# A hybrid decoder layer on one core: query rotation on VectorE alone, its copy on ScalarE, and projection work moved between stages

## The chip, the cores and the metric

The kernel runs on 1 core of one Trainium2 chip. Its time is the device time of one execution in microseconds (us). Five engines work side by side: TensorE (PE in the rows, its weight loads PEld), VectorE (DVE), ScalarE (ACT), GpSimd (POOL) and SyncE (SP, which only issues DMAs here). Each takes its own instructions in the order in which the program wrote them, and semaphores tie the engines together.

## The reference

One decoder layer over x of 512 tokens by 1024 features, all in float32. Cut to what matters here:

```
h    = rmsnorm(x, norm1_w);  proj = h @ w_in            # split into mq,mk,mv,mo,mi,mf,nq,kc..vw,ng,gm,gn
qk   = silu(causal_dwconv(concat(mq, mk)))              # 4 taps
hm   = rmsnorm(mlstm_chunkwise(mq, mk, mv, ...)) * sigmoid(mo)        # 4 heads
qn   = rope(rmsnorm(nq per head, q_norm_w))             # 8 heads x 64; the same for kc, ks, kw
on   = gated sum of compressed, selected and window attention (qn, k.., v..)
y    = sigmoid(gm + b0) * (hm @ w_up_m) + sigmoid(gn + b1) * (on @ w_up_n)
x    = x + y @ w_out
out  = x + (gelu(dwconv(a)) * v) @ ffn_w_down,   a, v = split(rmsnorm(x) @ ffn_w_up)
```

`rope(x)` takes the two halves x1, x2 of a head and gives x1*cos - x2*sin and x2*cos + x1*sin.

## The kernel before

Tokens are worked in four tiles of 128 (t = 0 to 3). Every float32 product is made of three matmuls over rounded halves (high x high, high x low, low x high), so one 128x512 piece of a projection is three matmuls of 512 columns. Such a triple is called a block here. Weights come from memory by SyncE into two buffers (`raw`), and are split into four rotating buffers (`whl`): ScalarE copies the high half (L88); the low half is a VectorE subtraction (L94), or, for A, gm, mo, mqk and gn, a second ScalarE copy (L91) and an accumulating DMA that GpSimd issues (L92). Each call of `ensure` issues these for one half chunk of weights.

The order is written out by hand. The attention and the mLSTM are a chain of small steps; between them stand calls `fill(ns)`, which take blocks out of one generator (`proj_stream`: the projections C, A = queries, MV, gm, mo, mqk, gn) until their nominal price, 650 ns a block, has paid the given number. A debt is carried on. The numbers come from a table, `PLAN`, read by `FL(key, default)`. `fill.until(done, flag)` takes blocks until a projection has been evacuated, and sets the debt to zero. A block that a `fill` takes early is missing later: the sum of blocks is fixed. A block also issues what hangs on its place in the stream: the weight splits of a half chunk three ahead, and evacuations (`after`, `tick`).

The places that the change touches, in time order:

- **Query tiles.** When A is done, `rope_norm` makes the scale of the query heads. Then for each tile: `rope` (L679 scale, L683 twice for the swapped half products with the sine, L686 product with the cosine, L687 sum, and a duplicate made by `cp`, L233 on ScalarE or L235 on VectorE) writes `qdup`; `q_transposes` (L846 on PE into `pq`, L848 on ScalarE and L849 on VectorE into `QS`) uses it. `rope_q(t + 1)` is issued right behind the transposes of tile t, and then `fill(z16_t)`. Keys in PLAN: `p_S1q*` and `p_dupq*` choose the engine (2 GpSimd, 1 VectorE, 0 VectorE for the product and ScalarE for the copy).
- **The rows of the mLSTM's gates** (`rows_b`), woven between attention heads; its last piece transposes them into `uop` (L1082).
- **After attention**: the convolved `mqk` is put through sigmoid (L1233), split into `mq` (L1240, L1243), then the sigmoids of `mo` (L1247) and `gm` (L1252), each with fills behind it; then ScalarE loads the function table for exponentials and logarithms (L1254).
- **mLSTM heads** h = 0 to 3: `mls_s` (scores, L1094 to L1104), `mls_e` (L1113), `mls_x` (exponential L1119, mask on GpSimd L1123), `mls_m` (L1128), `mls_b` (L1136 onwards, PE tile `mo`), `mls_c` (transposes `mhT` L1165, then L1166 to L1168). Fills `ms0`, `mb*`, `mc*`, `md*` stand between them; `mb3` is large enough to empty the stream.

Of the kernel before, what the change touches and what calls it, by code (L numbers as in the profile page):

```python
# [12 lines left out]
LNEXP = "natural_log_exp_and_others"  # L13
# [84 lines left out]
def bcast(ap, n):  # L98
# [3 lines left out]


PLAN = {
# [12 lines left out]
    "p_sc21": 0, "p_sc30": 0, "p_sc31": 1, "poolA": 2, "poolC": 0, "poolGM": 2, "poolGN": 2, "poolMO": 2,  # L117
    "poolMQK": 2, "poolMV": 0, "poolUM": 0, "poolUN": 2, "poolWO": 0, "q2_eb": 1, "q2_ex0": 0, "q2_ex1": 0,
# [8 lines left out]
}  # L127
# [1 line left out]
def FL(key, default):  # L129
    return PLAN.get(key, default)  # L130
# [30 lines left out]
def body(ctx, tc, I, out, dbg=None):  # L161
    nc = tc.nc
    act, dve, pe, pool = nc.scalar, nc.vector, nc.tensor, nc.gpsimd
# [24 lines left out]
    def sm(shape, name, bufs=2, dt=F32):  # L188
        return small.tile(shape, dt, name=name, tag=name, bufs=bufs)
# [7 lines left out]
    def page(name, dt=F32):  # L197
        return ar.tile([P, 2048], dt, name=name, tag="pg", bufs=PG)
# [7 lines left out]
    def s4(name, dt=F32):  # L206
        return ar.tile([P, 1024], dt, name=name, tag="s4", bufs=6)
# [7 lines left out]
    def pt(name):  # L215
        return ps.tile([P, 512], F32, name=name, tag="pt", bufs=1)
# [4 lines left out]
    def v4(tl):  # L221
        return tl[:, :2048].rearrange("p (k t) -> p k t", t=S)
# [520 lines left out]
    def proj_stream():  # L743
        yield from tok_group(T_C, 288, tok_accs("aC"), evac_c, "C")
        yield from tok_group(T_A, 512, tok_accs("aA"), evac_a, "A")
        T["mv1"] = lpage("mv1").rearrange("p (t h c) -> p t h c", t=NT, h=4)
        pool.memset(T["mv1"][:, :, :, P:P + 1], 1.0)
        yield from tok_group(T_MV, 512, tok_accs("aV"), evac_mv, "MV")
        T["gm"] = [v4(opage(f"gm{i}")) for i in range(2)]
        yield from feat_group(F_GM, gate_evac("gm", 0), "gm", "GM")  # L750
        T["mo"] = v4(page("mo"))
        yield from feat_group(F_MO, evac_mo, "mo", "MO")
        yield from feat_group(F_MQK, evac_conv, "mqk", "MQK")
        T["gn"] = [v4(page(f"gn{i}")) for i in range(2)]
        yield from feat_group(F_GN, gate_evac("gn", 8), "gn", "GN")

    fill = Filler(proj_stream(), flush)
# [271 lines left out]
    def rows_b():  # L1029
        ir, fr, t1, t2 = T["rows"]  # L1030

        act.activation(t1, fr, AF.Abs)
        act.activation(t1, t1, AF.Exp, scale=-1.0)
        dve.tensor_scalar(t2, fr, 0.0, None, op0=ALU.min)
        yield
        act.activation(t1, t1, AF.Ln, bias=1.0)
        yield
        dve.tensor_sub(fr, t2, t1)
        on = onesf[0:4, :]
        for c in range(NT):  # L1040
            q = slice(c * P, (c + 1) * P)
            dve.tensor_tensor_scan(t2[:, q], on, fr[:, q], 0.0, ALU.mult, ALU.add)
        yield
        dve.tensor_sub(ir, ir, t2)
        mc = sm([4, 4], "mc", 1)
        for c in range(NT):
            q = slice(c * P, (c + 1) * P)
            dve.tensor_tensor_scan(fr[:, q], on, ir[:, q], mc[:, c:c + 1] if c else 0.0, ALU.mult, ALU.max)
            if c + 1 < NT:
                e = (c + 1) * P - 1  # L1050
                dve.tensor_add(mc[:, c + 1:c + 2], t2[:, e:e + 1], fr[:, e:e + 1])
        yield

        dve.tensor_add(t1, t2, fr)
        R3 = s4("mrowC", F32R)
        nH, nL = R3[0:4, 0:512], R3[32:36, 0:512]
        pool.tensor_scalar(R3[0:32, 0:512].rearrange("p (a c) -> p a c", a=4),
                           onesf[0:32, :].rearrange("p (o c) -> p o c", o=1).to_broadcast([32, 4, P]), 0.0, None,
                           op0=ALU.mult)
        dve.tensor_scalar(fr, fr, -1.0, None, op0=ALU.mult)  # L1060
        dve.tensor_copy(nH, fr)
        dve.tensor_sub(nL, fr, nH)
        T["nHL"] = R3[0:36, 0:512]
        yield "R4"

        R4 = vst[:, 1024:1792]
        n = 0
        T["urow"] = []
        for k, (i, j) in enumerate(pairs):
            if i == j:  # L1070
                cur = ir[:, j * P:(j + 1) * P]
            else:
                new = R4[0:4, n * P:(n + 1) * P]
                n += 1
                dve.tensor_scalar(new, cur, t2[:, i * P - 1:i * P], None, op0=ALU.add)
                cur = new
            T["urow"].append(cur)

        yield
        p = pt("uop")  # L1080
        for k in range(len(pairs)):
            pe.transpose(p[:, k * 4:k * 4 + 4], T["urow"][k], ident[0:4, 0:4])  # L1082
        for t in range(NT):
            pe.transpose(p[:, 40 + t * 4:44 + t * 4], T["rows"][2][:, t * P:(t + 1) * P], ident[0:4, 0:4])
        dve.tensor_copy(uoc, p[:, 0:40])
        act.activation(emc, p[:, 40:56], AF.Exp, scale=-1.0)

    def mls_s(h):
        r0 = slice((h % 2) * 64, (h % 2) * 64 + 64)
        mq = T["mq"][h // 2][r0]  # L1090
        A = psS(f"mA{h}")
        B = psS(f"mB{h}")
        mb = B[:, 0:512]
        pe.matmul(mb, sel[:, h, :], T["nHL"], start=True, stop=True)  # L1094
        at = [A[:, 0:512], A[:, 512:896], B[:, 768:1024], B[:, 512:768]]
        for j in range(NT):
            ks = slice(j * P, (j + 1) * P)
            kh, kl = mq[:, 1, ks], mq[:, 3, ks]

            q0 = min(j, NT - 2) * P  # L1100
            qh, ql = mq[:, 0, q0:], mq[:, 2, q0:]
            pe.matmul(at[j], kh, qh, start=True, stop=False)
            pe.matmul(at[j], kh, ql, start=False, stop=False)
            pe.matmul(at[j], kl, qh, start=False, stop=True)  # L1104
        return A[:, 0:896], B[:, 640:1024], mb

    def mls_e(h, sc):
        mb = sc[2]
        EA, EB = s4(f"EA{h}"), s4(f"EB{h}")
        et = [EA[:, 0:512], EA[:, 512:896], EB[:, 128:384], EB[:, 0:128]]  # L1110
        for k, (i, j) in enumerate(pairs):
            e = et[j][:, (i - j) * P:(i - j + 1) * P]
            dve.tensor_scalar(e, mb[:, i * P:(i + 1) * P], uoc[:, k * 4 + h:k * 4 + h + 1], 0.0,  # L1113
                              op0=ALU.add, op1=ALU.min)
        return EA[:, 0:896], EB[:, 0:384], et

    def mls_x(ee):
        EA, EB, et = ee
        act.activation(EA, EA, AF.Exp)  # L1119
        act.activation(EB, EB, AF.Exp)  # L1120
        for j in range(NT):
            e = et[j][:, 0:P]
            pool.affine_select(e, e, pattern=[[1, P]], compare_op=ALU.is_ge, fill=0.0, base=0,  # L1123
                               channel_multiplier=-1)
# [124 lines left out]
    for i in range(2):  # L1249
        for z in range(2):  # L1250
            g = T["gm"][i][:, 2 * z:2 * z + 2, :]
            act.activation(g, g, AF.Sigmoid)  # L1252
            fill(FL("z26", 1300))
    act.preload_act_table_set(LNEXP)  # L1254
    T["hmH"] = v4(page("hmH", F32R))
    sc = mls_s(0)
    ee = mls_e(0, sc)
    mls_x(ee)
    fill(FL("ms0", 5000))
    mls_m(sc, ee)  # L1260
    for h in range(4):
        if h < 3:
# [5 lines left out]
        if h == 3:  # L1268
            fill.until(done, "GN")
            fill = Filler(up_group(F_UN, T["onH"], T["onL"], evac_un, "un", "UN"), flush)  # L1270
# [33 lines left out]
    fill = Filler(up_group(F_UM, T["hmH"], T["hmL"], evac_um, "um", "UM", psS), flush)  # L1304
# [336 lines left out]
```

## Time and profile before

| what | us |
|---|---|
| median of 3 runs (800.81 to 802.07) | 801.13 |
| the profiled execution's own time | 799.94 |
| its span in the trace | 798.2 |
| PE busy in the span | 776.9 (97%) |
| PEld busy | 640.9 |
| DVE busy | 469.7 |
| ACT busy | 373.0 |
| POOL busy | 211.1 |

PE counts as busy from the start of a matmul to its modelled end, and matmuls overlap, so the 97% says that PE is seldom without work, not that every cycle is used. The times of waits are read from the list of waits, which says for which engine an instruction waited last.

### The profile page before, as it was taken

What the parts mean: (1) busy time and instruction counts of PE and PEld (TensorE: products, weight loads), DVE (VectorE), ACT (ScalarE), POOL (GpSimd) and SP (SyncE); (2) the same over time, 40 slices, a digit from 0 to 9 for tenths busy, and PEclk for the clock granted to TensorE, in tenths of its full rate; (3) what the DMA queues carried; (4) which work ended last, traced back from release to release, by engine and by line L of the source; (5) the groups of instructions that cost most, each with busy time, mean ns of one, the idle gap of its engine ahead of it and who ended that gap; (6) DMA issues with size and microseconds to landing.
All of it is one profiled execution on the core that took longest, in us unless ns stands there. A gap on an engine that the chain in (4) does not pass through costs nothing.

```text
span 798.2 us, 10535 instructions
## 1 busy us (share of the span) xinstructions
PE 776.9 (97%) x4037; PEld 640.9 (80%) x4037; DVE 469.7 (59%) x825; ACT 373.0 (47%) x629; POOL 211.1 (26%) x219
## 2 busy tenths in 40 slices
PE   8999989999999999988999999999999999999998
PEld 5897878778788878866778998888888888888886
DVE  5476875686565654534764545555545544466865
ACT  6353546645565596571343343343343343355541
POOL 5320121220111122121000009855554444200600
PEclk9999999999999999999999999999999999999999
DMA  7884158665555567348343427675454444485472
GB/s 234 290 222 133 25 135 132 109 113 96 106 106 107 106 106 129 83 106 263 105 151 125 148 106 290 241 260 209 182 188 181 188 158 159 168 306 177 144 233 93
DMA packets 94371, 127.98 MB, mean 160 GB/s; under 512 B 6479, under 2 KB 73199, under 8 KB 92912
## 3 DMA queue, kind: packets, MB, share of 16 engines
q1 hardware_dynamic: 63054, 91.64, 34.3%
q0 software_dynamic: 31264, 35.66, 21.6%
q8 instruction: 32, 0.52, 0.3%
q14 instruction: 19, 0.16, 0.1%
q10 hardware_dynamic: 2, 0.00, 0.0%
HBM read 94.79 MB, written 15.73 MB: 138 GB/s over the span
## 4 chain that ended last, share of the span: by engine, by line
PE 79%; DVE 9%; ACT 6%; DMA 3%; issue 2%; SPq 0%; DVEq 0%; ACTq 0%
PE ff L1356 10%; PE ff L1357 10%; PE ff L1358 10%; PE P L426 4%; PE P L427 4%; PE P L425 4%; PE on L946 2%; PE ptp L935 2%; PE wo L425 2%; PE wo L426 2%; PE wo L427 2%; PE gm L487 1%; PE gm L489 1%; PE gm L488 1%; PE sp L905 1%
## 5 line engine op out<-in xcount | busy, mean ns | idle before, releaser
L94 DVE TENSOR_TENSOR whl<-raw,whl 128x1024 fp32r<-128x1024 f32 (+1 forms) x110 | 138.9, 1276 | 146.7 <-ACT whl L88 146.7
L88 ACT ACTIVATE whl<-raw 128x1024 fp32r<-128x1024 f32 (+2 forms) x144 | 144.8, 1013 | 125.7 <-PE ff L1358 57.0
L1356 PE MATMUL ff<-h2H,whl 128*128 128x512 f32 (+1 forms) x384 | 142.8, 372 | 0.0
L1357 PE MATMUL ff<-h2L,whl 128*128 128x512 f32 (+1 forms) x384 | 142.6, 371 | 0.0
L1358 PE MATMUL ff<-h2H,whl 128*128 128x512 f32 (+1 forms) x384 | 142.6, 371 | 0.0
L92 POOL DMA_DIRECT2D whl<-raw x32 | 46.2, 1444 | 198.5 <-ACT whl L91 190.3
L1358 PEld LDWEIGHTS ff<-h2H,whl 128*128 128x128 f32 x384 | 72.3, 188 | 12.6
L1356 PEld LDWEIGHTS ff<-h2H,whl 128*128 128x128 f32 x384 | 72.3, 188 | 12.5
L1357 PEld LDWEIGHTS ff<-h2L,whl 128*128 128x128 f32 x384 | 72.3, 188 | 12.3
L920 ACT ACTIVATE P<-sp,nmx 128x128 f32<-128x128 f32 (+3 forms) x64 | 33.1, 524 | 36.7 <-DVE nmx L911 36.4
L1408 ACT ACTIVATE ct<-ct 128x512 f32<-128x512 f32 x22 | 14.0, 634 | 54.4 <-DVE ct L1406 54.4
L911 DVE TENSOR_REDUCE nmx<-sp 128x2 f32<-128x256 f32 (+3 forms) x32 | 26.2, 818 | 17.9 <-PE sp L908 17.8
L426 PE MATMUL P<-whl,g 128*128 128x512 f32 x88 | 34.2, 389 | 0.0
L427 PE MATMUL P<-whl,g 128*128 128x512 f32 x88 | 34.2, 389 | 0.0
L425 PE MATMUL P<-whl,g 128*128 128x512 f32 x88 | 34.2, 389 | 0.0
L1406 DVE SCALAR_TENSOR_TENSOR ct<-ff,vcol,ct 128x511 f32<-128x511 f32 (+1 forms) x44 | 32.8, 744 | 2.5 <-ACT ct L1404 1.7
L91 ACT ACTIVATE whl<-raw 128x1024 fp32r<-128x1024 f32 x32 | 33.6, 1050 | 0.0
L1414 ACT ACTIVATE g<-ct 128x512 fp32r<-128x512 f32 x22 | 13.9, 634 | 37.0 <-DVE ct L1418 21.9
L235 DVE COPY P<-ptp 128x256 f32<-128x256 f32 (+1 forms) x32 | 17.7, 554 | 19.3 <-PE ptp L935 19.2
L1415 DVE TENSOR_TENSOR g<-ct,g 128x512 fp32r<-128x512 f32 x22 | 15.4, 699 | 22.0 <-ACT g L1414 22.0
L425 PE MATMUL wo<-whl,yH 128*128 128x512 f32 x64 | 25.2, 394 | 1.8 <-DVE gm L1299 1.8
L487 PE MATMUL gm<-hTH,whl 128*128 128x512 f32 x64 | 26.6, 416 | 0.0
(400 smaller groups left out, 1788.6 us busy)
## 6 DMA issues: line engine op xcount, KB each, us to landing
raw<-in_ffn_w_up_dram SPq DMA_DIRECT2D x22, 1024.0 KB, 5.0
raw<-in_w_in_dram SPq DMA_DIRECT2D x16, 1024.0 KB, 5.0
whl<-raw POOLq DMA_DIRECT2D x32, 512.0 KB, 5.7
st<-in_ffn_w_down_dram SPq DMA_DIRECT2D x11, 1024.0 KB, 6.9
td<-st POOLq DMA_DIRECT2D x11, 1024.0 KB, 4.1
raw<-td SPq DMA_DIRECT2D x22, 512.0 KB, 5.4
raw<-in_ffn_w_down_dram SPq DMA_DIRECT2D x11, 512.0 KB, 4.4
raw<-in_w_out_dram SPq DMA_DIRECT2D x4, 1024.0 KB, 11.0
```

Of the source, the lines that this page charges most:

```text
L88: nc.scalar.activation(h, src, AF.Copy)
L91: nc.scalar.activation(l, src, AF.Copy, scale=-1.0)
L92: nc.gpsimd.dma_start(l, src, accum_op=ALU.add)
L94: (nc.gpsimd if n in self.on_pool else nc.vector).tensor_sub(l, src, h)
L425: pe.matmul(o, aH, bH, start=start, stop=False)
L426: pe.matmul(o, aH, bL, start=False, stop=False)
L427: pe.matmul(o, aL, bH, start=False, stop=stop)
L487: pe.matmul(acc, H[:, k, :], hh, start=(k == 0), stop=False)
L920: act.activation(Pv[:, y], sv[:, y], AF.Exp, bias=nmx[:, y:y + 1], accum_out=den[:, y:y + 1])
L1356: pe.matmul(acc[:, a:b], H[:, k, :], hh, start=(k == 0), stop=False)
L1357: pe.matmul(acc[:, a:b], H[:, k, :], hl, start=False, stop=False)
L1358: pe.matmul(acc[:, a:b], L[:, k, :], hh, start=False, stop=(k == KD - 1))
```

## The change

Numbers of PLAN and three places of code. In PLAN: the evacuation of query tile 2 goes from VectorE to ScalarE (`e_a2` 1 to 0); the second sine product of all query tiles from GpSimd to VectorE (`p_S1q0` to `p_S1q3`, 2 to 0); the duplicate of tiles 0 to 2 from VectorE to ScalarE (`p_dupq0` to `p_dupq2`, 1 to 0; tile 3 had it there); the fills around the query tiles grow (`z14` 5850 to 6500, `z16_0` 4225 to 4875, `z16_1` 3250 to 4550, `z16_2` 4875 to 5525); the fills behind the mLSTM's heads shrink (`md0` 3950 to 3300, `md1` 3625 to 2600, `md2` 15275 to 0). In code: a `fill(650)` ahead of the transposes of `uop`; the table load for the exponentials goes from ahead of `mls_s(0)` to behind the first half of fill `ms0`, and `mls_x` of head 0 with it.

```
-    "mc0": 4675, "mc1": 5000, "mc2": 5000, "mc3": 11500, "md0": 3950, "md1": 3625, "md2": 15275, "ms0": 6300,
+    "mc0": 4675, "mc1": 5000, "mc2": 5000, "mc3": 11500, "md0": 3300, "md1": 2600, "md2": 0, "ms0": 6300,
...
-    "z13": 650, "z14": 5850, "z16_0": 4225, "z16_1": 3250, "z16_2": 4875, "z16_3": 2925, "z18": 1300, "z18a": 1950,
+    "z13": 650, "z14": 6500, "z16_0": 4875, "z16_1": 4550, "z16_2": 5525, "z16_3": 2925, "z18": 1300, "z18a": 1950,
...
         yield
+        fill(650)
         p = pt("uop")
...
-    act.preload_act_table_set(LNEXP)
     T["hmH"] = v4(page("hmH", F32R))
     sc = mls_s(0)
     ee = mls_e(0, sc)
+    fill(FL("ms0", 5000) / 2)
+    act.preload_act_table_set(LNEXP)
     mls_x(ee)
-    fill(FL("ms0", 5000))
+    fill(FL("ms0", 5000) / 2)
     mls_m(sc, ee)
```

What this does to the order of PE, counted in blocks (triples of matmuls), before and after: 16 and 17 ahead of the transposes of query tile 0 (from the last key transposes), 7 and 8 behind them, 5 and 7 behind those of tile 1, 7 and 8 behind those of tile 2; one block more ahead of `uop`; 18 and 12 between the last attention product and `mls_s(0)`; 10 and 10 between `mls_s(0)` and the first product of head 0; 7 and 7 ahead of the transposes `mhT` of head 0, 6 and 5 behind them; 8 and 8, 6 and 5 for head 1; 8 and 7, 4 and 7 for head 2. The other counts are the same.

The first place is ScalarE around query tiles 0 and 1: `qdup` is a tile's rotated queries, `whl` a half chunk of weights being split, `pq` the transposes in PSUM. Before:

```order
L383 ACTIVATE rs_l_974<-rs_l_974 128x32
L88 ACTIVATE whl_991<-raw_740 128x1024
L88 ACTIVATE whl_1020<-raw_910 128x1024
L91 ACTIVATE whl_1020<-raw_910 128x1024
L848 ACTIVATE QS_859<-pq_1027 128x512
L848 ACTIVATE QS_859<-pq_1034 128x512
L848 ACTIVATE QS_859<-pq_1070 128x512
L848 ACTIVATE QS_859<-pq_1077 128x512
L233 ACTIVATE vst<-sc_1092 128x256
L88 ACTIVATE whl_1104<-raw_910 128x1024
L91 ACTIVATE whl_1104<-raw_910 128x1024
```

The same place after:

```order
L383 ACTIVATE rs_l_974<-rs_l_974 128x32
L233 ACTIVATE qdup_983<-qdup_983 128x8x64
L88 ACTIVATE whl_991<-raw_740 128x1024
L88 ACTIVATE whl_1020<-raw_910 128x1024
L91 ACTIVATE whl_1020<-raw_910 128x1024
L848 ACTIVATE QS_859<-pq_1030 128x512
L848 ACTIVATE QS_859<-pq_1037 128x512
L233 ACTIVATE qdup_1044<-qdup_1044 128x8x64
L88 ACTIVATE whl_1070<-raw_910 128x1024
L91 ACTIVATE whl_1070<-raw_910 128x1024
L848 ACTIVATE QS_859<-pq_1080 128x512
L848 ACTIVATE QS_859<-pq_1087 128x512
```

The copy of each tile now stands ahead of the weight splits of the fill that follows it, and those ahead of the copies L848 of the same tile's transposes. Tile 2 reads likewise, with the score copy `vst<-sc` and two splits between.

The second place is ScalarE where attention ends: `onH` is the last output of attention, `cv` the convolution input of the mLSTM, `cs` its sigmoid. Before:

```order
L233 ACTIVATE P_7_2700<-ptp_7_1_2757 128x512
L956 ACTIVATE onH<-on_2378 128x4x128
L728 ACTIVATE cv_2731<-mqk_2727,vcol 128x512
L1233 ACT_TABLE_LOAD
L1233 ACTIVATE cs_2814<-cv_2522 128x1024
```

After:

```order
L728 ACTIVATE cv_2675<-mqk_2671,vcol 128x512
L233 ACTIVATE P_7_2730<-ptp_7_1_2779 128x512
L956 ACTIVATE onH<-on_2402 128x4x128
L1234 ACT_TABLE_LOAD
L1234 ACTIVATE cs_2814<-cv_2458 128x1024
```

The last evacuation of `mqk` now stands inside attention, and the table load directly behind `onH`. What follows it, up to the sigmoids of `gm`, is the same in both.

The third place is ScalarE at the exponential of head 0 (`EA`, `EB`), behind the sigmoids of `gm`. Before:

```order
L1252 ACTIVATE gm_1200<-gm_1200 128x1024 x2
L1254 ACT_TABLE_LOAD
L1119 ACTIVATE EA_2896<-EA_2896 128x896
L1120 ACTIVATE EB_2897<-EB_2897 128x384
L718 ACTIVATE gn_2793<-gn_2834,vcol 128x512
L88 ACTIVATE whl_2931<-raw_2733 128x1024
```

After:

```order
L1253 ACTIVATE gm_1180<-gm_1180 128x1024 x2
L718 ACTIVATE gn_2769<-gn_2834,vcol 128x512
L1259 ACT_TABLE_LOAD
L1120 ACTIVATE EA_2895<-EA_2895 128x896
L1121 ACTIVATE EB_2896<-EB_2896 128x384
L88 ACTIVATE whl_2931<-raw_2677 128x1024
```

One evacuation of `gn` went ahead of the table load and the two exponentials.

## Rows read from the trace of the kernel before

**Rows 1.** Busy time by stretch: engines, then clock, DMA share, GB/s.

```profile
280.00:300.00 20.00, 19.37 (x89) 15.33 (x88) 11.20 (x21) 19.96 (x24) 4.16 (x6) 1.00 0.61 106
...
376.00:404.00 28.00, 22.95 (x92) 17.94 (x91) 21.71 (x30) 7.83 (x12) 0.00 (x0) 0.94 0.22 75
```

**Rows 2.** Waits of PE: us in total, times, longest.

```profile
PE pq L846 <- DVE qdup L235: 1.8, 3, 1.0
...
PE gn L487 <- ACT gn L718: 0.6, 1, 0.6
PE mo L1136 <- DVE EA L1128: 0.6, 1, 0.6
PE pq L846 <- ACT qdup L233: 0.6, 1, 0.6
PE uop L1082 <- DVE P L235: 0.5, 1, 0.5
```

**Rows 3.** Line 686: duration ns min/median/max, first and last start.

```profile
L686 DVE TENSOR_TENSOR rtq<-qraw,tab x4: 1223/1228/1230, 93.4 to 112.8; 128x512 f32<-128x512 f32 x4
...
L686 DVE TENSOR_TENSOR rtk<-kraw,tab x1: 685/685/685, 67.8 to 67.8; 128x512 f32<-128x512 f32 x1
```

**Rows 4.** Timeline of POOL in query tile 1: start, us, instruction, idle before.

```profile
99.51 0.96 POOL L683 TENSOR_TENSOR rtq<-qraw,tab 128x256 f32<-128x256 f32 x1 [3.14 <-DVE qraw L679]
```

**Rows 5.** Timeline of DVE: a key rotation, then query tile 1.

```profile
66.43 0.69 DVE L679 TENSOR_TENSOR kraw<-kraw,rrs 128x512 f32<-128x512 f32 x1
...
68.55 0.69 DVE L687 TENSOR_TENSOR kdup<-rtk 128x512 f32<-128x512 f32 x1
...
98.73 0.69 DVE L679 TENSOR_TENSOR qraw<-qraw,rrs 128x512 f32<-128x512 f32 x1
...
99.80 1.22 DVE L686 TENSOR_TENSOR rtq<-qraw,tab 128x512 f32<-128x512 f32 x1
101.12 0.69 DVE L687 TENSOR_TENSOR qdup<-rtq 128x512 f32<-128x512 f32 x1
```

**Rows 6.** Timeline of ACT around the query tiles.

```profile
91.31 2.20 ACT L88 ACTIVATE whl<-raw 128x1024 fp32r<-128x1024 f32 x2
...
96.78 1.09 ACT L848 ACTIVATE QS<-pq 128x512 fp32r<-128x512 f32 x2 [2.32 <-PE pq L846]
...
104.86 1.05 ACT L88 ACTIVATE whl<-raw 128x1024 fp32r<-128x1024 f32 x1
105.81 1.05 ACT L91 ACTIVATE whl<-raw 128x1024 fp32r<-128x1024 f32 x1
...
114.84 0.63 ACT L233 ACTIVATE qdup<-qdup 128x512 f32<-128x512 f32 x1 [3.98 <-DVE qdup L687]
```

**Rows 7.** Timeline of PE: transposes of query tiles 0, 1 and 3.

```profile
96.12 1.06 PE L846 MATMUL pq<-ident,qdup 128*128 128x128 f32 x8 [0.31 <-DVE qdup L235]
...
102.43 1.06 PE L846 MATMUL pq<-ident,qdup 128*128 128x128 f32 x8 [0.46 <-DVE qdup L235]
...
115.52 1.09 PE L846 MATMUL pq<-ident,qdup 128*128 128x128 f32 x8 [0.57 <-ACT qdup L233]
```

**Rows 8.** Timeline of ACT from the end of attention to head 0.

```profile
276.67 0.60 ACT L956 ACTIVATE onH<-on 128x512 fp32r<-128x512 f32 x1 [2.00 <-PE on L946]
...
279.75 1.28 ACT L1233 ACT_TABLE_LOAD   x1
...
296.52 0.95 ACT L1119 ACTIVATE EA<-EA 128x896 f32<-128x896 f32 x1
...
297.79 0.67 ACT L718 ACTIVATE gn<-gn,vcol 128x512 f32<-128x512 f32 x1
```

**Rows 9.** Timeline of PE there: first block, head 0's scores, its products.

```profile
276.55 0.50 PE L487 MATMUL mqk<-hTH,whl 128*128 128x512 f32 x1
...
289.06 0.50 PE L1094 MATMUL mB<-mrowC,sel 36*128 36x512 f32 x1
...
299.37 0.46 PE L1136 MATMUL mo<-mv,EA 128*128 128x129 f32 x2
```

6 rows, old and new, of the table PLAN are left out of this document.

## The prediction

> **What bounds the kernel now.** I read the busy times first: PE is busy nearly throughout, so the kernel can only change by what PE waits, since the change neither adds nor removes a matmul. The list of waits comes second. In the stretches that the change touches, PE waits 1.8 and 0.6 us for the rotated queries, 0.5 us at `uop`, 0.6 us for an evacuation of `gn`, and 0.6 us for the exponentials of head 3 [rows 2]: 4.1 us in all, which is the most that can be won there. Third come the timelines, to see which engine ends last at each of these waits. Two things are to be seen. At the query tiles a loop runs through three engines: PE transposes, ScalarE copies (L848), VectorE subtracts and rotates the next tile, a copy makes the duplicate, PE transposes again [rows 5 to 7]. And behind attention ScalarE is the full engine: 19.96 of 20 us from 280 to 300 [rows 1], with PE just keeping pace.
>
> A block (three matmuls) costs 0.695 us: 18 blocks lie between 276.55 and 289.06 [rows 9].
>
> **Rotation on VectorE.** VectorE's product L686 takes 1.23 us in the query tiles and 0.685 us in the key rotation that leaves GpSimd out [rows 3]; in tile 1 it starts at 99.80 while GpSimd's half product runs from 99.51 to 100.47 [rows 4, 5]. GpSimd's half goes to VectorE. The row for the result is the key rotation: 66.43 to 68.55 + 0.69 = 69.24, so 2.81 us, against 98.73 to 101.81, 3.08 us, for the query tile [rows 5]. Saved: 0.27 us a tile.
>
> The Trainium skill (SBUF — State Buffer, the vocabulary entry on the shared port pair) says that GpSimd and VectorE lock a port pair for a whole instruction and the loser stands still. By that L686 would end at 100.47 + 0.685 = 101.16; the row ends at 101.02, 0.14 us sooner. Had the rule its full price, the removal would be worth 0.41 us a tile instead of 0.27 and the total some 0.4 us lower; I go by the rows.
>
> **The copy on ScalarE.** Tile 3 has it already: the copy starts at 114.84, takes 0.63, and PE starts at 115.52, so 0.68 us from copy to transposes, and 0.72 with the hop to ScalarE. Tile 1 with VectorE's copy: rotation done at 101.81, PE at 102.43, 0.62 us [rows 5 to 7]. Added: 0.10 us a tile.
>
> What counts more is what is queued behind it. ScalarE takes its instructions in order, and a copy that waits for the rotation now holds the weight splits written after it; the order shows them between the copy and L848 of the same tile. Before, three splits of tile 0 ran from 91.31 on, while VectorE rotated, and ScalarE then stood idle until 96.78; the next two ran at 104.86 and 105.81, behind L848 of tile 1 and off the loop [rows 6]. A split costs 0.95 us start to start [rows 6]. From L848 to the next rotation takes 98.73 - 96.78 = 1.95 us [rows 5, 6].
>
> Tile 0: its transposes started at 96.12 with VectorE's copy; by the two steps above the copy is done 0.27 sooner and 0.10 later, near 95.85. PE comes one block later than its arrival now, 96.12 - 0.31 + 0.69 = 96.5, and does not wait. ScalarE splits three times: 95.85 + 2.85 = 98.70, where L848 begins, almost 2 us later than now. Then 1.95 + 2.81 + 0.72 = 5.48 us to the next transposes: 104.2. Tile 1, two splits: 104.15 + 1.90 + 5.48 = 111.5. Tile 2, two splits and the score copy (0.3, an estimate from half of the 0.63 row, which moves twice as much): 111.5 + 2.2 + 5.48 = 119.2. In the kernel before, tile 3 is transposed at 115.52; the four blocks added from tile 0 on and one before it are 5 x 0.695 = 3.5 us of work done earlier, so 119.0 would be no loss. **Term: +0.2 us.** Bounds: -2.4 if all query waits go [rows 2], which needs the splits off the loop; +0.9 if a split costs the 1.05 us of a whole row [rows 6]. I take the value near the start-to-start row.
>
> The evacuation of tile 2 on ScalarE is costed at nothing: it takes the place of one of two VectorE copies ahead of `rope_norm`, and ScalarE's four squares and VectorE's four sums behind it overlap. If that cover failed it would be one 0.63 us copy [rows 6] on the loop's start, within the bound above.
>
> **`uop`.** One block ahead of its transposes gives VectorE's copy 0.69 us, and 0.5 was waited [rows 2]. **Term: -0.5 us** (0 if something else holds it).
>
> **From attention to head 0.** Six blocks fewer stand between the last attention product and `mls_s(0)` (18 to 12), since five went to the query tiles and one to `uop`. PE therefore asks for head 0's products 6 x 0.695 = 4.2 us sooner, counted from 276.55. What must be ready is ScalarE's: two sigmoids of `cv`, `mq`, `mo`, `gm`, the table load, EA. Before, the chain starts with the load at 279.75, behind the evacuation of the last `mqk`; after, that evacuation lies inside attention, and the load follows `onH`, which ends at 276.67 + 0.60 = 277.27 [rows 8]. So the chain starts 2.5 us sooner. Splits, sigmoids and copies in it are the same. At its end one evacuation of `gn` (0.67 us [rows 8]) now goes ahead of the load and EA: EA comes 2.48 - 0.67 = 1.8 us sooner, near 294.7. Head 0's products follow EA by 299.37 - 296.52 = 2.85 us [rows 8, 9], through GpSimd's mask and VectorE's product, so they start near 297.6. PE alone could be there at 299.37 - 4.2 - 0.6 = 294.6; the 0.6 us wait for `gn` goes, and one of 3 us in all takes its place, split between the scores (which need `mq`) and the products. 4.2 us of work left this stretch, and it gets 1.8 us shorter. **Term: +2.4 us.** Bounds: -0.6 (ScalarE keeps pace and the `gn` wait goes) and +4.2 (the chain starts no sooner). I take the value of the ScalarE rows, because that engine has 0.04 us of slack in 20 [rows 1].
>
> **The heads.** Blocks move from behind heads 0 and 1 and ahead of `mhT` of head 2 (one each) to behind `mhT` of head 2 (4 to 7). The 0.6 us wait for head 3 goes. Three places lose a block, and PE meets its partners there with next to no wait in the list today, so each may open a wait between 0 and 0.69 us. **Term: +0.1 us** (0.7 of new waits, a third of the most, less 0.6), between -0.6 and +1.5. `md2` to 0 itself moves no work of PE: `mb3` takes the same blocks directly behind it. From head 3 on, the sigmoids of `gn`, the table loads and the transfers of `w_up_m` hang on head 3's products by the same chain as before, and the stage shifts as a whole.
>
> **Sum.** +0.2 - 0.5 + 2.4 + 0.1 = +2.2 us. The profiled execution took 799.94 us (span 798.2, 1.7 around it) and would take 802.1; it lies 1.2 us under the median of the runs shown, 801.13, which would become **803.3 us**, 0.27% slower.
>
> **The rivals.**
> - *Faster: VectorE's free time decides.* The five blocks cover the query loop, and ScalarE keeps pace behind attention. For it: VectorE's chain does get shorter by 0.27 us a tile, and every added block is longer than the wait it meets. Against it: the splits stand in the loop, and ScalarE is full. It decides from the point at which the loop of a tile takes less than PE's 8 blocks and transposes, about 6.7 us (19.4 us from 96.12 to 115.52, less some 2.1 of waits, plus 4 blocks, over three tiles [rows 2, 7]). Then the waits of rows 2 go but for head 3's: -2.4 - 0.5 - 0.6 = -3.5, 797.6 us.
> - *No change: one of the two stages behaves.* If the query waits go and the gate stage loses as I say: -2.4 - 0.5 + 2.4 + 0.1 = -0.4, 800.7. If the query stage is as I say and ScalarE's chain has slack that a busy row hides, the third term is near 0: -0.2, 800.9. This is also the case in which blocks merely trade places.
> - *Slower still: the clock.* After a wait of PE the granted clock can fall to its lower level of 1.2 GHz: the stretch from 376 to 404 has a mean of 0.94 [rows 1], which costs 28 x 0.06 = 1.7 us of full-speed work. New waits of 1 to 2 us ahead of head 0 could do the same in the stretch from 280 to 300, at 1.00 now. Against it: the query waits of up to 1.0 us [rows 2] did nothing of the kind. 803.3 + 1.7 = 805.0 us.
>
> **How the numbers follow.** The forecast has 0.50, the faster rival 0.13, no change 0.27, the clock 0.10. This kernel's measurement tells 0.2%, 1.6 us, from no change: faster is under 799.5, slower over 802.7. Of the forecast's own spread (802.2 to 804.4), about a tenth lies under 802.7, so slower has 0.45 + 0.10 = 0.55, the same 0.05 + 0.27 = 0.32, faster 0.13. The range reaches down through the no-change cases and up to the clock's: 800.0 to 805.0.
>
> **What would show it.** Right: in the changed profile PE still waits about 2.5 us for `qdup`, all of it named ScalarE; L848 starts behind two or three splits; L686 takes 0.685 us; the wait at `uop` is gone; between `onH` and EA ScalarE has no idle time, EA starts 17.4 us behind `onH`'s end, and PE waits some 3 us for `mq` and EA. Wrong: query waits under 1 us with L848 on time, or head 0's products right behind their blocks.

## The result, and the profile after

The changed kernel takes 811.96 us (median of 4 runs, 811.28 to 812.65), the kernel before 801.60 beside it on the same chip (4 runs, 800.81 to 802.62): a ratio of 1.0129, 95% interval 1.0111 to 1.0146. It is 10.4 us slower. 803.3 was forecast, with a range up to 805.0; the sign is right and the size is not.

The first view that I read is the time at which PE reaches the same instruction in both traces, since PE is the engine that everything else only delays.

| PE starts | before | after | later by |
|---|---|---|---|
| transposes of query tile 0 | 96.12 | 96.86 | 0.74 |
| transposes of query tile 3 | 115.52 | 119.31 | 3.79 |
| scores of attention tile 3, head 1 | 230.74 | 235.01 | 4.27 |
| scores of attention tile 3, head 7 | 266.13 | 276.62 | **10.49** |
| scores of mLSTM head 0 (`mB`) | 289.06 | 295.76 | 6.70 |
| products of mLSTM head 0 (`mo`) | 299.37 | 308.30 | 8.93 |
| first product of `un` | 344.80 | 354.56 | 9.76 |
| first product of `um` | 371.83 | 383.00 | 11.17 |
| first product of the last group (`P`, L425) | 688.80 | 700.07 | 11.27 |

The trace's span grew by 11.6 us (798.2 to 809.8), the medians by 10.4. Of the 3.79 us at query tile 3, 3.5 are five blocks of work done earlier; they and the block at `uop`, 4.2 us together, are missing ahead of `mB`. What stands out is one attention tile that loses 6.2 us between its second and its last head. It is a stretch of which the prediction says nothing.

The list of PE's waits after (us in total, times, longest) names what is new there:

```profile
PE on L946 <- ACT P L233: 3.1, 3, 1.0
...
PE pq L846 <- ACT qdup L233: 2.4, 3, 1.2
...
PE on L893 <- DVE onL L957: 1.7, 2, 1.2
...
PE mo L1137 <- DVE EA L1129: 1.4, 1, 1.4
PE mA L1103 <- ACT mq L1241: 1.1, 1, 1.1
PE gn L487 <- ACT gn L718: 0.8, 1, 0.8
```

Against [rows 2]: the waits for the rotated queries are still 2.4 us in all and now all ScalarE's, the one at `uop` is gone, and three places that the list of before does not have hold 3.1, 1.7 and 1.1 us. The lines for `mo` and `gn` name other places than before: `mo` waited ahead of head 3's products (342.58) and now waits ahead of head 0's (308.30), `gn` waited ahead of head 0 and now waits ahead of `mhT` of head 2. The first line is PE waiting for ScalarE's copy of the attention weights P. The timeline of ScalarE after shows what that copy stood behind, between the scores of heads 2 and 3 of tile 3 (start, us, instruction; in brackets idle time and releaser; `cv<-mqk` is an evacuation, `whl<-raw` a split):

```profile
245.34 0.68 ACT L920 ACTIVATE P<-sp,nmx 128x512 f32<-128x512 f32 x1
...
246.00 0.78 ACT L728 ACTIVATE cv<-mqk,vcol 128x512 f32<-128x512 f32 x1
246.67 1.06 ACT L88 ACTIVATE whl<-raw 128x1024 fp32r<-128x1024 f32 x1
247.61 1.06 ACT L91 ACTIVATE whl<-raw 128x1024 fp32r<-128x1024 f32 x1
248.56 0.60 ACT L233 ACTIVATE P<-ptp 128x512 f32<-128x512 f32 x1
```

The timeline of PE after, at the same place:

```profile
246.90 1.30 PE L946 MATMUL on<-P,vst 128*64 128x128 f32 x18
249.21 1.09 PE L946 MATMUL on<-P,vst 128*64 128x128 f32 x14 [1.01 <-ACT P L233]
```

And the same evacuation and splits in the kernel before, where they come between the scores of heads 3 and 4 (L920, the exponential, belongs to the scores of head 4 here, and to those of head 2 above):

```profile
247.44 0.60 ACT L233 ACTIVATE P<-ptp 128x512 f32<-128x512 f32 x1 [0.17 <-PE ptp L935]
247.93 0.78 ACT L728 ACTIVATE cv<-mqk,vcol 128x512 f32<-128x512 f32 x1
248.60 1.06 ACT L88 ACTIVATE whl<-raw 128x1024 fp32r<-128x1024 f32 x1
249.54 1.06 ACT L91 ACTIVATE whl<-raw 128x1024 fp32r<-128x1024 f32 x1
250.50 0.69 ACT L920 ACTIVATE P<-sp,nmx 128x512 f32<-128x512 f32 x1
```

The evacuation, the two splits and the durations are the same; what they stand ahead of is not. Before, the copy that PE needs next goes first and 2.6 us of work that nobody needs yet goes behind it, into ScalarE's free time. After, the evacuation and the two splits go first. They hang on blocks, and the blocks had moved six places, which is a head and a half. A half chunk of `mqk` weights is eight blocks, which are two heads of tile 3, so the collision comes back at every second head: 1.0 us at each of three `on`, and 1.2 near the start of the tile, where `onH` stands behind two splits. These four waits are 4.3 of the 6.2 us. The list counts a wait from the modelled end of the matmul before it, and matmuls overlap: from start to start the four places lose 4.9 us, and the rest is in steps of 0.2 us and less, which the list does not have.

The stages of the prediction, after. Rotation, line 686 (duration ns min/median/max, first and last start):

```profile
L686 DVE TENSOR_TENSOR rtq<-qraw,tab x4: 682/684/689, 94.3 to 117.1; 128x512 f32<-128x512 f32 x4
```

ScalarE at query tile 1, with two splits between the copy and L848 that stood behind L848 before [rows 6]:

```profile
103.89 0.63 ACT L233 ACTIVATE qdup<-qdup 128x512 f32<-128x512 f32 x1 [3.71 <-DVE qdup L687]
104.42 1.04 ACT L88 ACTIVATE whl<-raw 128x1024 fp32r<-128x1024 f32 x1
105.37 1.04 ACT L91 ACTIVATE whl<-raw 128x1024 fp32r<-128x1024 f32 x1
106.32 1.06 ACT L848 ACTIVATE QS<-pq 128x512 fp32r<-128x512 f32 x2
```

ScalarE from the end of attention to head 0, which answers to [rows 8]:

```profile
287.45 0.60 ACT L956 ACTIVATE onH<-on 128x512 fp32r<-128x512 f32 x1 [2.01 <-PE on L946]
288.07 1.28 ACT L1234 ACT_TABLE_LOAD   x1
...
305.39 0.95 ACT L1120 ACTIVATE EA<-EA 128x896 f32<-128x896 f32 x1
```

PE there, which answers to [rows 9]:

```profile
295.76 0.50 PE L1095 MATMUL mB<-mrowC,sel 36*128 36x512 f32 x1
...
308.30 0.91 PE L1137 MATMUL mo<-mv,EA 128*128 128x129 f32 x6 [1.43 <-DVE EA L1129]
```

Last, two windows of the changed kernel in which PE ran at its lower level of 1.2 GHz (stretch; busy time of PE, PEld, DVE, ACT, POOL; granted clock, DMA share, GB/s):

```profile
370.00:372.00 2.00, 2.00 (x6) 1.52 (x6) 0.06 (x1) 0.00 (x0) 1.00 (x2) 0.50 1.14 145
...
414.00:416.00 2.00, 2.00 (x6) 1.52 (x6) 1.75 (x2) 2.00 (x3) 0.00 (x0) 0.50 0.04 8
```

The kernel before has one such spell behind the heads, from 378 to 384, inside the stretch with 0.94 of [rows 1]; the changed kernel has two. Each takes about 1.7 us of full-speed work.

### The profile page after: what moved, and what is told of

The parts are those of the page before. It is cut to its first block, busy times and chain, and to the rows that moved or that the text cites. A ratio compares the mean times of both kernels' runs of the same rounds, so it can differ in the third digit from the quotient of the medians.

```text
span 809.8 us, 10527 instructions
## 1 busy us (share of the span) xinstructions
PE 781.7 (97%) x4037; PEld 642.0 (79%) x4037; DVE 466.1 (58%) x825; ACT 373.5 (46%) x633; POOL 206.8 (26%) x215
## 4 chain that ended last, share of the span: by engine, by line
PE 75%; DVE 11%; ACT 9%; issue 2%; DMA 2%; POOL 0%; ACTq 0%; DVEq 0%; SPq 0%; POOLq 0%
PE ff L1358 10%; PE ff L1360 10%; PE ff L1359 10%; PE P L426 4%; PE P L427 4%; PE P L425 4%; ACT whl L88 2%; PE wo L425 2%; PE wo L426 2%; PE wo L427 2%; PE on L946 2%; PE ptp L935 1%; DMA raw<-in_w_up_m_dram 1%; ACT P L920 1%; DVE nmx L911 1%
## 5 line engine op out<-in xcount | busy, mean ns | idle before, releaser
L920 ACT ACTIVATE P<-sp,nmx 128x128 f32<-128x128 f32 (+3 forms) x64 | 33.1, 524 | 48.8 <-DVE nmx L911 48.6
L425 PE MATMUL P<-whl,g 128*128 128x512 f32 x88 | 34.2, 389 | 0.0
L425 PE MATMUL wo<-whl,yH 128*128 128x512 f32 x64 | 25.8, 403 | 1.8 <-DVE gm L1301 1.8
L487 PE MATMUL gn<-hTH,whl 128*128 128x512 f32 x64 | 26.1, 408 | 0.8 <-ACT gn L718 0.8
```

The costliest lines, as they stand in the source:

```text
L425: pe.matmul(o, aH, bH, start=start, stop=False)
L920: act.activation(Pv[:, y], sv[:, y], AF.Exp, bias=nmx[:, y:y + 1], accum_out=den[:, y:y + 1])
```

## The experiments

Two theories. **Theory 1, a queue:** what costs the time is the place of the splits and evacuations that ride on the moved blocks. **Theory 2, the reassignment:** ScalarE's added copies and VectorE's added products cost it by crowding these engines. The kernel before ran at 801.8 to 802.0 beside all of these.

**The rotation and the copies alone**, no block moved:

```
-"e_a2": 1, "p_S1q0..3": 2, "p_dupq0..2": 1
+"e_a2": 0, "p_S1q0..3": 0, "p_dupq0..2": 0
```

> Theory 1 (the blocks moved ahead carry weight splits and evacuations with them; in the last attention tile these now stand on ScalarE directly ahead of the copy of P that PE needs, which costs 1.0 to 1.2 us at every second head): without the moved blocks nothing changes in attention, so the last attention tile takes what it took before (35.4 us from the start of sp25 to that of sp31), and what is left is the query loop, bound by ScalarE's splits and without blocks to cover them: about 3.4 us longer, near 805. Theory 2 (VectorE's rotation and ScalarE's added copies themselves cost the time, by crowding these engines): most of the 10 us is there, 808 or more. A query loop as in the kernel before, with a total near 801, would speak against the price that I gave the splits.

Measured: 804.73 us, ratio 1.0037 (1.0023 to 1.0052). In attention PE is 4.60 us late at the first scores and 4.61 at the last: nothing is lost there, so theory 2 falls as an account of the 6.2 us. The query loop is 3.6 us longer in the trace, as expected, but not all for the expected reason. L848 of tile 0 stood behind three splits, PE waited 2.3 us for the next copy, and then ran at the lower level:

```profile
108.00:110.00 2.00, 2.00 (x8) 1.81 (x8) 1.95 (x5) 0.00 (x0) 0.00 (x0) 0.50 0.00 0
```

From tile 0 to tile 1 it lost 1.85 us to the splits, from tile 1 to tile 2 2.0 us at 1.2 GHz with no split in the loop.

**The five blocks alone:**

```
-"z14": 5850, "z16_0": 4225, "z16_1": 3250, "z16_2": 4875
+"z14": 6500, "z16_0": 4875, "z16_1": 4550, "z16_2": 5525
```

> The five blocks moved from the stretch behind attention to the query tiles, rotation and copies as before, no block at uop. Theory 1: the attention work meets the blocks five of eight further on, and in this phase the splits do not stand directly ahead of the copy of P that PE's next product needs, so the last attention tile loses under 2 us; the query waits go (-2.4), the stretch from attention to head 0 loses about 1: 800 to 802. Theory 2: no added copies, so no loss, near 799. Should the last attention tile lose 5 us or more here, the phase that I read from the order is wrong.

Measured: 803.88 us, 1.0024 (1.0013 to 1.0035), above the 800 to 802 of theory 1. The query waits are gone from the list, as expected. But the last attention tile loses 3.4 us (1.10 late at head 1, 4.54 at head 7), where I had expected under 2. I had looked at ScalarE's queue only; in this phase the collision is on VectorE, where two of the three pieces of an evacuation of `mqk` (L731) go ahead of a copy of P:

```profile
248.09 1.52 DVE L731 SCALAR_TENSOR_TENSOR cv<-mqk,vcol,cv 128x511 f32<-128x511 f32 x2
249.53 0.68 DVE L235 COPY P<-ptp 128x512 f32<-128x512 f32 x1
```

In the kernel before these three pieces come one head later, and behind the copy:

```profile
250.32 0.68 DVE L235 COPY P<-ptp 128x512 f32<-128x512 f32 x1
250.92 2.31 DVE L731 SCALAR_TENSOR_TENSOR cv<-mqk,vcol,cv 128x511 f32<-128x511 f32 x3
```

PE, which needs the PSUM tile that this copy empties:

```profile
250.27 0.66 PE L935 MATMUL ptp<-ident,P 128*128 128x128 f32 x4 [0.85 <-DVE P L235]
```

So moved blocks without any reassignment cost the attention tile too, and the rows say by the same mechanism on another engine. The stretch from there to head 0's products lost 2.7 us in this trace where about 1 was expected; a spell at 1.2 GHz stood in it (0.50 from 296 to 298).

**The splits six blocks later**, on the changed kernel:

```
-"q8_ensMQK": 1
+"q8_ensMQK": 7
```

> The changed kernel with one number altered: the splits of mqk's weights are asked for six blocks later, so that they stand behind the copy of P on ScalarE, as in the kernel before, while the evacuation of mqk stays ahead of it. Theory 1: the waits for P shrink from 1.0 to 1.2 us to at most 0.4 each, and the last attention tile gets 4 to 5.5 us shorter: near 807. Theory 2: ScalarE does the same work, so no gain: 811 to 812.5.

Measured: 807.07 us, 1.0069 (1.0049 to 1.0089): 4.9 us back for one number, with ScalarE's work unchanged. The wait for P on ScalarE is gone from the list, and in the trace the last attention tile loses 0.5 us instead of 6.2; 1.5 us of that are lost again up to head 0's products, where this trace has a spell at 1.2 GHz (0.50 from 294 to 298). ScalarE at a later head, with the copy ahead of the splits again:

```profile
252.78 0.60 ACT L233 ACTIVATE P<-ptp 128x512 f32<-128x512 f32 x1 [0.46 <-PE ptp L935]
253.27 1.05 ACT L88 ACTIVATE whl<-raw 128x1024 fp32r<-128x1024 f32 x1
254.22 1.05 ACT L91 ACTIVATE whl<-raw 128x1024 fp32r<-128x1024 f32 x1
```

**Two more blocks, to a whole period of eight:**

```
-"z16_3": 2925
+"z16_3": 4225
```

> The changed kernel with two more blocks ahead of attention's last tiles, so that its blocks stand eight, one whole period of two heads, further on than before; ScalarE's order around the copy of P is then that of the kernel before again. Theory 1: the 6.2 us lost in the last attention tile come back, and with two blocks fewer behind attention PE waits up to 1.4 us more for head 0: 806 to 807.5. Theory 2: no gain, or 1.4 us of loss: 812 to 813.5.

Measured: 809.05 us, 1.0091 (1.0072 to 1.0109): theory 1 by sign, outside its numbers. The attention tile is whole again (6.48 us late at head 1, 6.48 at head 7), so all 6.2 us came back, and ScalarE has the order of before:

```profile
253.92 0.60 ACT L233 ACTIVATE P<-ptp 128x512 f32<-128x512 f32 x1 [0.17 <-PE ptp L935]
254.41 0.77 ACT L728 ACTIVATE cv<-mqk,vcol 128x512 f32<-128x512 f32 x1
255.08 1.06 ACT L88 ACTIVATE whl<-raw 128x1024 fp32r<-128x1024 f32 x1
```

But from head 7 of the last attention tile to the first product of head 1 it lost 5.5 us in the trace where the changed kernel lost 2.9: PE waited 3.3 us for EA instead of 1.4, and then ran at 1.2 GHz (0.50 from 304 to 306), so that head 0's products took 3.9 us instead of 2.4. Attention tiles 0 to 2 lost 0.6 us more than in the changed kernel. I had counted 1.4 for the two blocks.

**The third part alone** (heads and table load), on the kernel before:

```
-"md0": 3950, "md1": 3625, "md2": 15275      +"md0": 3300, "md1": 2600, "md2": 0
 (and the table load behind half of ms0, as in the change)
```

> The kernel before with the third part of the change alone: the table load moved behind half of the blocks that stand ahead of head 0's exponentials, and fewer blocks behind the heads 0 to 2 (the blocks go behind the last head instead). Theory 1 takes from the two traces that the heads lose about 0.8 us (the changed kernel lost 0.9 from head 0's products to the first up-projection): 802 to 803.5 against 801.7. The rival, that the table load put behind blocks is what makes PE wait 1.1 and 1.4 us ahead of head 0 in the changed kernel: then the stretch from the last attention product to head 0's products gets 1 to 2.5 us longer here too, and the total is 803.5 to 805.

Measured: 803.24 us, 1.0017 (1.0006 to 1.0028). From head 0's scores to the first product of `un` it loses 1.3 us in the trace: 0.55 ahead of head 0's products (PE waits 1.4 us for EA there, where the kernel before waited 0.6 us for an evacuation of `gn` one block earlier) and 0.75 in the heads, with the wait of 0.8 us for `gn` that the changed kernel has. Behind attention, up to head 0's scores, nothing is lost. The rival's 1 to 2.5 us did not come.

**The copy of P on VectorE**, on the changed kernel:

```
-"e_pt31": 0
+"e_pt31": 1
```

> The changed kernel with one number altered: the copy of P's second half in the last attention tile goes from ScalarE to VectorE (eight copies), and everything else, the splits ahead of it included, stays. Theory 1 (the loss is a queue: the copy waits behind two splits and an evacuation that nobody needs yet): the 3.1 us of waits for that copy go, the 1.7 us of waits for the rounded attention output stay, 808 to 809.5. Rival (the last attention tile is short of ScalarE's or VectorE's time as a whole): moving work to VectorE, which is the busier of the two there, gains nothing, 811 to 813.

Measured: 807.88 us, 1.0083 (1.0065 to 1.0102), 4.1 us less than the changed kernel, and a little better than expected. The splits are where they were; the copy no longer stands behind them. VectorE took eight copies more, and PE's list has no wait for them. What is left in that tile is the wait at its start:

```profile
PE on L893 <- DVE onL L957: 1.6, 2, 1.1
```

**Rotation on VectorE with the copy left there, and a borrowed block at `uop`**, on the kernel before:

```
-"p_S1q0..3": 2
+"p_S1q0..3": 0
+        fill(650)
         p = pt("uop")
...
+        fill(-650)        # behind the transposes
```

> The kernel before with two parts of the change in a form that moves no split: the rotation all on VectorE, its copy left where it was (VectorE in tiles 0 to 2, ScalarE in tile 3), and one block ahead of the transposes of uop that is given back right behind them, so that every block from there on stands where it stood. Theory 1: 0.27 us of rotation saved in each of three loops and 0.5 us of wait at uop, nothing lost elsewhere: 1.3 us less, 800.3 against 801.7. If the rotation on VectorE costs something by itself (its products crowd VectorE in the query tiles), no change or up to 1 us more: 801.5 to 802.7.

Measured: 800.24 us, 0.9985 (0.9973 to 0.9996): a little faster than the kernel before, and much faster than the changed one. The waits of the queries fall from 2.4 to 1.2 us:

```profile
PE pq L846 <- DVE qdup L235: 0.9, 3, 0.4
...
PE pq L846 <- ACT qdup L233: 0.3, 1, 0.3
```

From the first experiment (2.95 us over the kernel before, this one 1.7 under it) it differs in the copies' engine, the evacuation of tile 2 and the block at `uop`, which is worth 0.6; so the copies on ScalarE, with the splits that they hold and the clock behind them, cost about 4 us when no block covers them, if the evacuation of tile 2, which was not run by itself, costs nothing.

**Five blocks from tile 1 instead of from behind attention**, added to that:

```
-"z14": 5850, "z16_0": 4225, "z16_1": 3250, "z16_2": 4875, "f3_1": 1000
+"z14": 6500, "z16_0": 4875, "z16_1": 4550, "z16_2": 5525, "f3_1": 594
```

> The kernel before with the rotation on VectorE and the borrowed block at uop as in the run before, and with the five more blocks in the query tiles, which are now taken from the heads of attention tile 1 and not from the stretch behind attention: from tile 2 on every block, with its splits, stands where it stood in the kernel before. Theory 1: the query waits of 2.4 us go, the last attention tile and the stretch behind it are as before, and only tile 1 may lose, since it has five blocks fewer: 798 to 800.5. If it was the blocks in the query tiles as such that cost time (they crowd ScalarE there), 802 to 804.

Measured: 804.84 us, 1.0040 (1.0026 to 1.0053), against the forecast. The last tile loses nothing, but tile 1 has one wait of 4.4 us. ScalarE there, with the second copy of a split:

```profile
174.09 1.05 ACT L91 ACTIVATE whl<-raw 128x1024 fp32r<-128x1024 f32 x1
```

GpSimd, with the weight DMA that adds to that split:

```profile
175.49 1.55 POOL L92 DMA_DIRECT2D whl<-raw  x1 [12.64 <-ACT vst L233]
176.41 2.17 POOL L1057 TENSOR_SCALAR mrowC<-onesf 32x512 fp32r<-32x512 f32 x1
```

VectorE, with the copy of P as the last of three in its queue:

```profile
178.62 0.42 DVE L1061 CAST mrowC<-rowpg 4x512 fp32r<-4x512 f32 x1 [3.29 <-POOL mrowC L1057]
...
180.72 0.68 DVE L235 COPY P<-ptp 128x512 f32<-128x512 f32 x1
```

PE:

```profile
181.46 1.97 PE L946 MATMUL on<-P,vst 128*64 128x128 f32 x14 [4.44 <-DVE P L235]
```

A weight DMA had come ahead of the zeroing L1057, and through three queues the wait for its split reached PE. (The row of the DMA names the ScalarE copy right behind that split.) In the kernel before the zeroing stood ahead of that DMA:

```profile
166.00 2.18 POOL L1057 TENSOR_SCALAR mrowC<-onesf 32x512 fp32r<-32x512 f32 x1
176.19 1.58 POOL L92 DMA_DIRECT2D whl<-raw  x1 [8.01 <-ACT whl L91]
```

Behind the wait the clock was granted at 0.50 from 180 to 186.

**The same, with the blocks given back by head 4 of tile 1**, so that GpSimd has its old order at L1057:

```
-            fill(f3[n])
+            fill(f3[n] - (650 if 8 <= n < 13 else 0))     # "f3_1" back at 1000
```

> As the run with five blocks taken from attention tile 1, but all five are given back by head 4 of that tile (one each behind heads 0 to 4). In that run PE waited 4.4 us once: a weight DMA on GpSimd, which waits for a split, had come ahead of the zeroing L1057, VectorE's cast waited for the zeroing, and the copy of P behind the cast waited with it. Here GpSimd has its order of the kernel before again at L1057. Theory 1 (queues): that wait goes, with the slow clock behind it, and the gain of the query stage is kept: 798 to 799.8 against 801.9. Rival (tile 1 cannot spare five blocks, the wait only shows where PE runs out of them): a wait of 3 us or more somewhere in tile 1 stays, 802 to 805.

**The same, with the blocks taken from tile 0:**

```
-"f3_0": 1300
+"f3_0": 894                                               # "f3_1" back at 1000
```

> The same with the five blocks taken from the eight heads of attention tile 0 instead of tile 1. Theory 1: tile 1 and all behind it have the order of the kernel before, so no wait of 4.4 us at L1057; tile 0 has only three blocks a head (650 and 1300 of budget), and with five of 24 gone its heads, 2.7 to 3.4 us each, may wait for their exponentials: 798.5 to 801. Rival (the blocks in the query tiles cost time as such): 802 or more.

**The blocks as in the run with the wait, the zeroing one step earlier:**

```
         yield
+        R3 = ...; pool.tensor_scalar(R3[0:32, 0:512], ..., 0.0)
         dve.tensor_sub(ir, ir, t2)
...
         dve.tensor_add(t1, t2, fr)
-        R3 = ...; pool.tensor_scalar(R3[0:32, 0:512], ..., 0.0)
```

> The run with the wait of 4.4 us again, its blocks unchanged, with one instruction moved: GpSimd's zeroing of mrowC is written one step earlier, ahead of the weight DMA that it stood behind. Theory 1: the wait and the slow clock behind it go, 798 to 800. Rival (tile 1 is short of blocks, whatever the order on GpSimd): as that run, 803.5 to 806.

Measured, all against the kernel before at 801.96: given back early 799.96 us, 0.9972 (0.9959 to 0.9985); from tile 0 **799.05 us, 0.9964 (0.9953 to 0.9974)**; the zeroing earlier 800.68, 0.9983 (0.9969 to 0.9996). In all three the wait of 4.4 us is gone and no query wait is left. The first and the third are 0.2 and 0.7 us over what I expected. In the trace of the first, PE comes 1.8 us later out of tile 1 than five blocks less would make it, with a new wait of 0.9 us for exponentials, so tile 1 does pay for part of them. In the trace of the third it pays 2.4 us, with two new waits for P of 1.9 us in all: moving the one instruction gave 4.2 us back between the medians (804.84 to 800.68), and the rival, that tile 1 is short of blocks, holds for the rest. Tile 0 pays 0.7. The version from tile 0 is the fastest that was run. Whether it beats the first of the three is not settled, since their intervals overlap.

## Why the prediction was wrong

Per stage, from the traces, with the blocks that were moved counted out at 0.695 us each:

| stage | forecast | measured |
|---|---|---|
| up to the queries | 0 | +0.5 |
| query tiles | +0.2 | -0.2 |
| `uop` | -0.5 | -0.6 |
| attention, tiles 0 to 2 | not named | +0.4 |
| attention, last tile | **not named** | **+6.2** |
| attention to head 0's products | +2.4 | +2.6 |
| heads | +0.1 | +0.8 |
| behind the heads | 0 | +1.5 |

The lines add up to 11.2 us, 9.0 more than the 2.2 forecast; 6.2 of the 9.0 are the last attention tile.

**What failed** is the costing of moved blocks by their PE time alone. The prediction has terms for the places where blocks arrive and where they leave, and none for the stretch between, where each block only comes five or six places earlier. It calls this work done earlier and counts 0.695 us a block. But a block brings splits and evacuations with it, and those go into the queues of ScalarE, VectorE and GpSimd between instructions that did not move. The change's second piece of order even shows an evacuation that "now lies inside attention"; I used it to start the chain behind attention 2.5 us sooner and didn't ask what it now stood ahead of. All that the prediction had named as signs of being right came true, or nearly, and the time was still wrong, because none of these signs lies in that stretch. Four kinds of run show this cost: the splits moved away from the copy (4.9 us back), the copy moved away from the splits (4.1), the phase turned by a whole period (all 6.2 in that tile), and blocks given back before the tile (nothing lost in it). The first two alter one number of the changed kernel each, so the order of the queues is shown as the cause of the loss in this tile; of the other stages only the heads and the query tiles were run by themselves, and the rest was read from the traces.

**What held.** The query loop: line 686 takes 0.68 us instead of 1.23 [rows 3], and the rotation of tile 1 runs from 101.04 to 103.85, the 2.81 us forecast, 0.27 less than before; tiles 1 to 3 are transposed at 104.57, 111.78 and 119.31 against 104.2, 111.5 and 119.2. The waits there stay at 2.4 us and are ScalarE's. By the rule of the Trainium skill (SBUF — State Buffer, the vocabulary entry on the shared port pair), that the loser stands still, the prediction's estimate for taking GpSimd out was 0.41 us a tile; the trace gives 0.27, so the row was the better price. The block at `uop` brought 0.6. From attention to head 0, ScalarE has no idle time from `onH` to EA, EA starts 17.3 us behind `onH`'s end (17.4 forecast), the products 2.9 us behind EA (2.85), and PE's waits of 1.1 and 1.4 us stand where it said, 2.5 of 3 us. Luck was in the first experiment and not in this term: its query loop was expected to grow by 3.4 us from the splits and grew by 3.6, but the price of the splits fits only tile 0 (1.85), and the rest was the clock (2.0).

**What was mis-sized.** The heads: new losses of some 1.4 us instead of 0.7 (the 0.8 measured and the 0.6 of head 3's wait, which did go), above all for the evacuation of `gn` ahead of `mhT` of head 2, where a block was taken away (the 0.8 us in the list). The third part alone lost 1.3 us in the trace and 0.17% of the time, which bears the sign out.

**The rival of the clock** was looked for ahead of head 0, where the changed kernel has no slow spell in its trace; it has one more than before behind the heads, and its 1.7 us are about the 1.5 measured there. Between the two profiled executions lie 11.7 us (799.94 and 811.66) and between the medians 10.4, so this spell may belong to these executions and not to the change; that was not settled. In four of the experiments' traces (the five blocks alone, the splits later, the two more blocks, the copy of P on VectorE) a spell did come between 292 and 308, so the rival's mechanism is real at that place, and is not what made the 10.4 us. The 0.5 us at the start comes from a wait for `hTH` of 1.5 us instead of 1.0, in code that the change leaves alone; it was up to 2.2 us in other traces, so I take it for chance, which is not shown.

## What to carry to other kernels

When filler work is moved, follow not only the filler but what it issues: for each stage between the old and the new place, print the order of every engine that works in its queue and look at what now stands ahead of the instruction that the busiest engine needs next. Where filler and main work repeat with periods that fit (eight blocks, two heads), a bad phase (the place of the filler within that period) is paid every time round. Borrowed filler that is given back before the next delicate stage leaves the later order alone: the same five blocks in the query tiles were part of a loss of 10.4 us in one way, and of a gain of 2.9 us in the other.

## What the runs showed that I had not expected

A spell at 1.2 GHz stands behind some waits of PE and not behind others, and the length of the wait does not tell which. The wait of 2.5 us ahead of `un` is followed by one in the changed kernel (0.50 from 370 to 372) and by none in the kernel before; so is the wait of 1.8 us ahead of `wo` (0.50 from 414 to 416). In the run of the five blocks alone a spell came from 294 to 300 where the only wait of PE in the list between the end of attention and that spell was 0.4 us, and the prediction had held against its rival that waits of up to 1.0 us did nothing of the kind. The cost differs too: by the windows the spell behind the wait of 2.3 us in the query tiles (104 to 114) took about 3.4 us of full-speed work, and those behind the heads about 1.7. The spread of a few us between executions of one kernel is of the size of one or two such spells; that they are its cause was not shown.
